# The sums of four adaLN vectors on GpSimd in 512-column pieces, instead of VectorE in 1024-column pieces

## The chip, the cores and the metric

The kernel runs on one core of a Trainium2 chip. The metric is the device time of one execution in microseconds (us). Engines are named as in the profile: PE is TensorE, DVE is VectorE, ACT is ScalarE, POOL is GpSimd, and SP is the engine whose queue issues most DMAs.

## What is computed

One decoder layer for 256 tokens of 2048 channels, all in float32. Six adaLN vectors are one product of a conditioning vector with a 2048 x 12288 matrix; they shift, scale and gate the two sub-layers.

```python
mod = c_act @ w_mod[l].astype(f32) + b_mod[l].astype(f32)
shift1, scale1, gate1, shift2, scale2, gate2 = [t[:, None, :] for t in jnp.split(mod, 6, axis=-1)]
u = _rms(h, norm1_w[l]) * (1.0 + scale1) + shift1
proj = u @ w_in[l].astype(f32)
...
merged = (jax.nn.sigmoid(gate_a) * (o_a @ p_a[l].astype(f32))
          + jax.nn.sigmoid(gate_b) * (o_b @ p_b[l].astype(f32)))
h = h + gate1 * (merged @ w_out[l].astype(f32))
u = _rms(h, norm2_w[l]) * (1.0 + scale2) + shift2
ff = jax.nn.silu(u @ w_gate[l].astype(f32)) * (u @ w_up[l].astype(f32))
h = h + gate2 * (ff @ w_down[l].astype(f32))
```

`o_a` is the output of a stick-breaking attention, `o_b` that of a gated DeltaNet (a chunked recurrence with a triangular solve).

## The kernel before

All large products stream their weights. `run_jobs` goes through 648 steps of one block each: 256 rows by 512 columns of a weight matrix, 512 KB, in a tile `raw` (four buffers) that SP's queue loads. ACT rounds a block to float32r (`wh`), DVE takes the rest (`wl`, one subtraction of two SBUF tiles), and PE adds three products for each pair of parts into `acc`. ACT and DVE prepare a block three steps ahead (`SA`); the load of the block four further on is written behind `wl`, since it takes that block's buffer. A job has the activations as the stationary side (12 products of 512 columns in a step) or, with `chan`, the weights (24 products of 256 columns).

Between the products run smaller chains. The first third of the program is the gated DeltaNet (`gdn_chain`, `conv_chain`), whose many small steps on DVE, ACT and PE hang on one another, with four POOL steps for each group of heads for inverse roots (`rr`, `sso`); then comes the attention (`sb_chain`), then the output products, then the FFN.

Shift1 and scale1 are summed at the start and don't change here. The other four vectors are background tasks: shift2 (index 3), scale2 (4), gate1 (2), gate2 (5). `run_jobs` counts ticks, two in a step, and calls `pump_bg` for one background step every `bg_every` ticks, in the first call only from tick `bg_from`. In `mod_steps` a background step loads the next piece of `w_mod` (128 rows by 1024 columns, tile `wm`, 512 KB, two buffers) on SP's queue and adds the piece at hand, times its value of silu(c), to the accumulator `macc` on DVE (L120, in the helper `stt`; the first piece L194). One vector takes 32 pieces; four vectors 128. Then PE sums over partitions: `mod_cols` by transposes and sums on ACT, `mod_bcast` by two products with ones after a split on ACT and DVE.

The order in which each engine's queue holds its instructions is set ahead of the run by a scheduler that follows the program's order and its own forecast of when an instruction can start; on the chip each queue is strictly in that order.

Of the kernel before, what the change touches and what calls it, by code (L numbers as in the profile page):

```python
# [16 lines left out]
P = 128  # L17
# [9 lines left out]
RAWS = 4  # L27
MW = 1024
GROUPS = (0, 2, 1, 3)
# [4 lines left out]
NZ = 3  # L34
BGF = 200
BGE = 3
H2 = 5
# [56 lines left out]
def body(tc, cst, x, c, w_mod, b_mod, norm1_w, w_in, q_norm_w, k_norm_w, conv_w, a_log, dt_bias,  # L94
# [32 lines left out]

    # constants
    cs0 = cp.tile([P, 2 * P], F32, name="cs0")
# [40 lines left out]

    # adaLN vectors
    def mod_steps(i, acc, pool, width, bufs, row, cc=cc):
        v0 = i * D
        if row:
            nc.gpsimd.memset(acc, 0.0)
            nc.sync.dma_start(out=acc[0:1], in_=b_mod[v0:v0 + D].rearrange("(o d) -> o d", o=1))
        parts = [(k, j) for k in range(KT) for j in range(0, D, width)]
        tiles = {}

        def load(n):  # L180
            k, j = parts[n]
            t = pool.tile([P, width], F32, tag="mraw", name=f"wm{i}_{n}", bufs=bufs)
            nc.sync.dma_start(out=t, in_=w_mod[k * P:(k + 1) * P, v0 + j:v0 + j + width])
            tiles[n] = t

        load(0)
        for n, (k, j) in enumerate(parts):
            if n + 1 < len(parts):
                load(n + 1)
            t = tiles.pop(n)  # L190
            if k or row:
                stt(acc[:, j:j + width], t, cc[:, k:k + 1], acc[:, j:j + width], ALU.mult, ALU.add)
            else:
                nc.vector.tensor_scalar(out=acc[:, j:j + width], in0=t, scalar1=cc[:, 0:1], scalar2=None, op0=ALU.mult)  # L194
            yield

    def mod_cols(acc, o, bias):
        for j in range(4):
            b = bank("pb_mod")
            for i in range(4):  # L200
                tr(b[:, i * P:(i + 1) * P], acc[:, (4 * j + i) * P:(4 * j + i + 1) * P])
            for i in range(4):
                k = 4 * j + i
                # in place: only the sum is used
                act(b[:, i * P:(i + 1) * P], b[:, i * P:(i + 1) * P], AF.Copy, accum_out=o[:, k:k + 1])
            yield
        tt(o, o, bias, ALU.add)
        yield

    def mod_bcast(acc, o, pool):  # L210
        for j in range(4):
            sl = slice(j * 512, (j + 1) * 512)
            hi = pool.tile([P, 512], F32R, tag="c2", name="bch", bufs=4)
            lo = pool.tile([P, 512], F32R, tag="c2", name="bcl", bufs=4)
            nc.scalar.copy(out=hi, in_=acc[:, sl])
            tt(lo, acc[:, sl], f32(hi), ALU.subtract)
            yield
            b = bank("pb_bc")
            mm(b, onesr, hi, True, False)
            mm(b, onesr, lo, False, True)  # L220
            nc.scalar.copy(out=o[:, sl], in_=b)
            yield

    # chains of small steps that run between the products of the streams
    chains = deque()
# [39 lines left out]

    # streamed products: float32 operands as exact sums of two float32r parts
    def run_jobs(jobs, bg_every=0, outer=(), bg_from=0):
# [30 lines left out]
        for n, (j, q) in enumerate(steps):  # L298
# [14 lines left out]
            def beat(t):  # L313
                # between the products of half a k-step
                if own:
                    if t == SPA and n + SA < ns:
                        split_hi(n + SA)
                    if t == SPB and n + SA < ns:
                        split_lo(n + SA)
                    pump_conv()  # L320
                    pump(j.pump)
# [36 lines left out]

# [1 line left out]
    acc01 = big.tile([P, 2, D], F32, tag="s16", name="acc01")  # L360
# [8 lines left out]
    def load_smod(n):  # L369
        # shift1 and scale1  # L370
        for i in [i for i in loads if i not in smod][:max(0, n - len([i for i in smod if smod[i] is not None]))]:
            pi, g = i
            k0, kn = pieces[pi]
            c0, cn = k0 * P, kn * P
            kg = 4 // kn
            t = tps.tile([P, 2, kg, cn], F32, tag="smod", name="smod", bufs=SMB)
            src = w_mod[g * kg * P:(g + 1) * kg * P, 0:2 * D].rearrange("(k p) (v n) -> p v k n", p=P, v=2)
            if kg == 1:
                nc.gpsimd.dma_start(out=t[:, :, 0], in_=src[:, :, 0, c0:c0 + cn])
            else:  # L380
                for v in range(2):
                    nc.gpsimd.dma_start(out=t[:, v], in_=src[:, v, :, c0:c0 + cn])
            smod[i] = t
# [78 lines left out]

    # the modulated input, 512 channels at a time as the columns of w_mod come in
    def u_piece(pi):
# [26 lines left out]

# [1 line left out]
    def gdn_scalars():  # L493
# [60 lines left out]

    # steps of the tensor engine for one group of four heads by slot; the digit: chunk of 128 rows
    def gdn_slots():
# [27 lines left out]
    def gdn_chain(g, tl):  # L584
# [7 lines left out]
        U = sysv(wB[:, 0])  # L592
        # two systems side by side: their even blocks on 64 partitions each
        Tm = sysv(wB[:, 1, 0:512])
# [18 lines left out]
        hold = {}  # L613
        # blocks of 16 on the diagonal: their places in turn, then system, on partitions; columns and rows free
        Lt, Tt = wA[:, 0, 0:512], wA[:, 0, 512:1024]
# [16 lines left out]
        def gather():  # L632
            # of each 32 the two blocks' columns over one another
            for q in range(4):
                e = slice(32 * q, 32 * q + 32)
                j = 32 * q
                nc.scalar.copy(out=Lc[e], in_=L[e, :, j:j + BW])
                nc.vector.copy_predicated(out=Lc[e], mask=mk["par"][e, 1:2].bitcast(mybir.dt.uint32).unsqueeze(2).to_broadcast([32, 8, BW]),
                                          data=L[e, :, j + BW:j + 2 * BW])
# [6 lines left out]
        def stages(j0, j1):  # L646
            # in place: row j of the inverse is done, its part in the rows below
            for j in range(j0, j1):
                n = BW - 1 - j
                t = tmp[:, 0:2 * n * j].rearrange("p (c h r) -> p c h r", h=2, r=n)  # L650
                tt(t, Tb[:, j, :, j + 1:].unsqueeze(1).to_broadcast([P, j, 2, n]),
                   Tb[:, 0:j, :, j].unsqueeze(3).to_broadcast([P, j, 2, n]), ALU.mult)
                d = Tb[:, 0:j, :, j + 1:]
                tt(d, d, t, ALU.add)
# [12 lines left out]
        def take_even(c):  # L667
            # the even blocks' columns of L
            s = LEVELS[level[c]]
# [3 lines left out]
        def turn(c, part):  # L673
            # the even blocks of T, their rows in order without the odd ones
            s = LEVELS[level[c]]
# [10 lines left out]
        def step(op, c):  # L686
# [53 lines left out]
            if op == "KK":  # L740
# [4 lines left out]
                def lower():  # L745
                    # L holds minus the strict part (its upper part is not used)
                    for h, s in enumerate(sys):
                        stt(L[:, s], ph(b, h), nbrk2[:, s:s + 1], Dm[:, s], ALU.mult, ALU.mult)
# [45 lines left out]
            if op == "Y":  # L794
                # the last level: two blocks of 64
                b = bank("pb_X")
# [121 lines left out]

    # the first halves of the second group's sums wait in SBUF for the rest of the input
    part = []  # L920
# [45 lines left out]

# [1 line left out]
    oa = {}  # L968
# [121 lines left out]

    # adaLN vectors of the second half
    def mod_col_task(i, slot):
        acc = tph["tp"].tile([P, D], F32, tag="macc", name="macc", bufs=1)
        yield from mod_steps(i, acc, tph["tp"], MW, 2, False)
        yield from mod_cols(acc, mcols[:, slot], {3: bsh2, 4: bsc2}[i])

# [3 lines left out]

# [1 line left out]
    def z_done(n):  # L1102
# [109 lines left out]

# [1 line left out]
    def gate_task(i, key, cc):  # L1214
        acc = tq.tile([P, D], F32, tag="macc2", name="macc2", bufs=1)
        yield from mod_steps(i, acc, tq, 1024, 2, True, cc)
        st[key] = tq.tile([P, D], F32, tag="gbc", name=key, bufs=1)
        yield from mod_bcast(acc, st[key], tq)

# [21 lines left out]

# [1 line left out]
    def ffn_begin():  # L1243
# [15 lines left out]
        norm_apply(hn, mcols[:, 2], b2, st["u2h"], st["u2l"])  # L1259
        # silu(c) again, in the place of b2: gate2's sums come after the norm  # L1260
        cc2 = cp.tile([P, KT], F32, tag="gate", name="cc2", bufs=1)
# [86 lines left out]

    run_jobs(jobs, bg_every=6)
    drain()  # L1350
# [24 lines left out]
```

## Time and profile before

| what | value |
|---|---|
| time, median of 3 runs | 2090.61 us (2089.65, 2090.61, 2098.76) |
| span of the profiled execution | 2093.9 us, from its first to its last instruction |
| profiled execution's own time | not listed apart from its span |
| PE busy | 2003.8 us (96%) |
| DVE busy | 1351.5 us (65%) |
| ACT busy | 1033.3 us (49%) |
| POOL busy | 115.5 us (6%) |
| HBM read | 445.70 MB, 214 GB/s over the span |

A matmul's end is modelled in the profile, so PE counts as busy almost always; whether it runs at its pace is read from how many products fall in a stretch. The chain that ended last lies for 78% on PE and for 9% on DMA.

### The profile page before, as it was taken

How to read it: one execution, taken by the hardware profiler on the slowest of the kernel's cores; microseconds unless marked ns; L12 is line 12 of the kernel's file. 1: busy time of each engine (PE TensorE's matmuls, PEld its weight loads, DVE VectorE, ACT ScalarE, POOL GpSimd, SP SyncE). 2: the span in 40 equal slices, each digit the busy share in tenths (PEclk: the TensorE clock that was granted, in tenths of full speed). 3: DMA queues.
4: the chain of work that ended last, by engine and by line, in shares of the span. 5: the costliest groups of instructions: out<-in, count | busy, mean ns of one | idle time of the engine just before them, and what ended most of it. 6: DMA issues, size and time to landing. Idle time of an engine off the chain costs nothing.

```text
span 2093.9 us, 31884 instructions
## 1 busy us (share of the span) xinstructions
PE 2003.8 (96%) x12505; PEld 1795.5 (86%) x12505; DVE 1351.5 (65%) x1758; ACT 1033.3 (49%) x1678; POOL 115.5 (6%) x139
## 2 busy tenths in 40 slices
PE   1999999999999999999999999999999999999998
PEld 1899999987888788877888888898999889999987
DVE  4987989987558876667654555677545454445454
ACT  3346676675666567433454444533444333444432
POOL 4411011110000000000000000000000000000000
PEclk9899999999999999999999999999999999999999
DMA  8995664664658875888766665688666556666664
GB/s 308 386 333 183 188 200 123 192 206 148 188 164 264 294 225 153 261 290 289 224 190 192 189 218 192 194 296 280 209 183 181 188 194 187 186 183 181 185 211 138
DMA packets 208561, 449.90 MB, mean 215 GB/s; under 512 B 16101, under 2 KB 16536, under 8 KB 207896
## 3 DMA queue, kind: packets, MB, share of 16 engines
q1 hardware_dynamic: 198906, 413.25, 63.3%
q0 software_dynamic: 9504, 34.61, 4.4%
q8 instruction: 98, 1.61, 0.3%
q14 instruction: 53, 0.43, 0.1%
HBM read 445.70 MB, written 2.10 MB: 214 GB/s over the span
## 4 chain that ended last, share of the span: by engine, by line
PE 78%; DMA 9%; DVE 6%; issue 3%; ACT 3%; SPq 0%; POOL 0%; DVEq 0%; ACTq 0%
PE acc L114 71%; DMA wm<-in_w_mod 7%; DVE wl L117 2%; DMA crow<-in_conv_w 1%; DVE macc L120 1%; ACT wh L282 1%; DMA smod<-in_w_mod 1%; PE pb_mod L114 1%; PE pb_Q L114 1%; PE pb_u L136 1%; DMA raw<-in_w_in 0%; PE pb_X L114 0%; PE pb_z L114 0%; PE pb_oa L114 0%; DVE gw L117 0%
## 5 line engine op out<-in xcount | busy, mean ns | idle before, releaser
L117 DVE TENSOR_TENSOR wl<-raw,wh 128x1024 fp32r<-128x1024 f32 x648 | 789.6, 1223 | 516.5 <-ACT wh L282 514.6
L282 ACT CAST wh<-raw 128x1024 fp32r<-128x1024 f32 x648 | 679.6, 1050 | 834.0 <-PE acc L114 670.1
L114 PE MATMUL acc<-u2h,wl 128*128 128x256 f32 x1408 | 399.3, 284 | 4.9 <-DVE wl L117 4.9
L114 PE MATMUL acc<-u2h,wh 128*128 128x256 f32 x1408 | 398.5, 283 | 0.0
L114 PE MATMUL acc<-u2l,wh 128*128 128x256 f32 x1408 | 398.4, 283 | 0.0
L114 PE MATMUL acc<-wh,uh 128*128 128x512 f32 x768 | 307.1, 400 | 0.0
L114 PE MATMUL acc<-wl,uh 128*128 128x512 f32 x768 | 301.2, 392 | 2.0 <-DVE wl L117 2.0
L114 PE MATMUL acc<-wh,ul 128*128 128x512 f32 x768 | 300.2, 391 | 0.0
L114 PEld LDWEIGHTS acc<-u2h,wl 128*128 128x128 f32 x1408 | 270.2, 192 | 6.2 <-DVE wl L117 6.1
L114 PEld LDWEIGHTS acc<-u2h,wh 128*128 128x128 f32 x1408 | 270.3, 192 | 0.0
L114 PEld LDWEIGHTS acc<-u2l,wh 128*128 128x128 f32 x1408 | 270.3, 192 | 0.0
L114 PE MATMUL acc<-uh,wh 128*128 128x256 f32 x768 | 220.9, 290 | 1.6 <-ACT part L927 1.3
L114 PE MATMUL acc<-uh,wl 128*128 128x256 f32 x768 | 219.4, 287 | 0.0
L114 PE MATMUL acc<-ul,wh 128*128 128x256 f32 x768 | 219.0, 286 | 0.0
L114 PE MATMUL acc<-wh,ff 128*128 128x512 f32 x704 | 217.1, 389 | 0.0
L114 PEld LDWEIGHTS acc<-wl,uh 128*128 128x128 f32 x768 | 144.4, 188 | 34.5 <-DVE wl L117 4.1
L114 PEld LDWEIGHTS acc<-wh,ul 128*128 128x128 f32 x768 | 144.8, 189 | 27.2
L114 PEld LDWEIGHTS acc<-wh,uh 128*128 128x128 f32 x768 | 144.9, 189 | 26.8
L120 DVE SCALAR_TENSOR_TENSOR macc<-wm,cols,macc 128x1024 f32<-128x1024 f32 x92 | 117.8, 1283 | 65.7 <-DMA wm<-in_w_mod 65.2
L114 PEld LDWEIGHTS acc<-wh,ff 128*128 128x128 f32 x704 | 132.1, 188 | 27.3
L114 PEld LDWEIGHTS acc<-uh,wh 128*128 128x128 f32 x768 | 148.7, 195 | 2.8 <-ACT part L927 1.5
L114 PEld LDWEIGHTS acc<-ul,wh 128*128 128x128 f32 x768 | 149.3, 194 | 0.5
(289 smaller groups left out, 2493.1 us busy)
## 6 DMA issues: line engine op xcount, KB each, us to landing
raw<-in_w_in SPq DMA_DIRECT2D x286, 512.0 KB, 4.5
wm<-in_w_mod SPq DMA_DIRECT2D x128, 512.0 KB, 5.3
raw<-in_w_gate SPq DMA_DIRECT2D x88, 512.0 KB, 3.9
raw<-in_w_up SPq DMA_DIRECT2D x88, 512.0 KB, 3.7
raw<-in_w_down SPq DMA_DIRECT2D x88, 512.0 KB, 3.9
smod<-in_w_mod POOLq DMA_DIRECT2D x64, 512.0 KB, 11.2
raw<-in_p_a SPq DMA_DIRECT2D x32, 512.0 KB, 5.6
raw<-in_p_b SPq DMA_DIRECT2D x32, 512.0 KB, 4.0
```

Source lines behind the costliest of these rows:

```text
L114: nc.tensor.matmul(o, lhsT=lhsT, rhs=rhs, start=start, stop=stop, skip_group_check=True)
L117: nc.vector.tensor_tensor(out=o, in0=a, in1=b, op=op)
L120: nc.vector.scalar_tensor_tensor(out=o, in0=a, scalar=s, in1=b, op0=op0, op1=op1, **kw)
L136: nc.tensor.transpose(o, i, ident)
L282: nc.scalar.copy(out=wh, in_=raws[n])
```

## The change

`mod_steps` is replaced by `mod_parts`. A vector is summed 512 columns at a time: for each quarter of the columns all 16 row blocks, so that one vector takes 64 pieces of 256 KB, and four vectors 256. The accumulator is 128x512 with two buffers. A piece is multiplied by its value of silu(c) in place and then added, both on POOL (`tensor_scalar`, `tensor_tensor`). Loads run four pieces ahead (`MRA`) with six buffers (`MRB`). The sum over partitions of a quarter (`use`) follows its 16 pieces. The first call of `run_jobs` now pumps every two ticks from tick 80 (was three, from 200), the second every three (was six). The products, their splits and the loads of `raw` are as before; comments went too.

```diff
-MW = 1024
-BGF = 200
-BGE = 3
+BGF = 80
+BGE = 2
+BGD = 3
+MRA = 4
+MRB = 6
...
-    def mod_steps(i, acc, pool, width, bufs, row, cc=cc):
+    def mod_parts(i, pool, row, cc, use):
         v0 = i * D
-        if row:
-            nc.gpsimd.memset(acc, 0.0)
-            nc.sync.dma_start(out=acc[0:1], in_=b_mod[v0:v0 + D].rearrange("(o d) -> o d", o=1))
-        parts = [(k, j) for k in range(KT) for j in range(0, D, width)]
+        parts = [(q, k) for q in range(4) for k in range(KT)]
         tiles = {}
 
         def load(n):
-            k, j = parts[n]
-            t = pool.tile([P, width], F32, tag="mraw", name=f"wm{i}_{n}", bufs=bufs)
-            nc.sync.dma_start(out=t, in_=w_mod[k * P:(k + 1) * P, v0 + j:v0 + j + width])
+            q, k = parts[n]
+            t = pool.tile([P, 512], F32, tag="mraw", name=f"wm{i}", bufs=MRB)
+            nc.sync.dma_start(out=t, in_=w_mod[k * P:(k + 1) * P, v0 + q * 512:v0 + (q + 1) * 512])
             tiles[n] = t
 
-        load(0)
-        for n, (k, j) in enumerate(parts):
-            if n + 1 < len(parts):
-                load(n + 1)
+        for n in range(MRA):
+            load(n)
+        for n, (q, k) in enumerate(parts):
+            if n + MRA < len(parts):
+                load(n + MRA)
+            if k == 0:
+                acc = pool.tile([P, 512], F32, tag="macc", name="macc", bufs=2)
+                if row:
+                    nc.gpsimd.memset(acc, 0.0)
+                    nc.sync.dma_start(out=acc[0:1], in_=b_mod[v0 + q * 512:v0 + (q + 1) * 512].rearrange("(o d) -> o d", o=1))
             t = tiles.pop(n)
-            if k or row:
-                stt(acc[:, j:j + width], t, cc[:, k:k + 1], acc[:, j:j + width], ALU.mult, ALU.add)
-            else:
-                nc.vector.tensor_scalar(out=acc[:, j:j + width], in0=t, scalar1=cc[:, 0:1], scalar2=None, op0=ALU.mult)
+            first = k == 0 and not row
+            nc.gpsimd.tensor_scalar(out=acc if first else t, in0=t, scalar1=cc[:, k:k + 1], scalar2=0.0,
+                                    op0=ALU.mult, op1=ALU.add)
+            if not first:
+                nc.gpsimd.tensor_tensor(out=acc, in0=acc, in1=t, op=ALU.add)
             yield
...
-    run_jobs(jobs, bg_every=6)
+    run_jobs(jobs, bg_every=BGD)
```

The new order of the queues shows at three places. The first is SP's queue at the start of the DeltaNet, behind the load of the constants `cs`: `raw` is a streamed block, `wm` a piece of `w_mod`. Before:

```order
L183 DMA wm_0_5081<-in_w_mod 128x1024
L277 DMA raw<-in_w_in 128x2x512
L183 DMA wm_1_5083<-in_w_mod 128x1024
L277 DMA raw<-in_w_in 128x2x512
L183 DMA wm_2_5154<-in_w_mod 128x1024
L277 DMA raw<-in_w_in 128x2x512 x2
L183 DMA wm_3_5204<-in_w_mod 128x1024
L277 DMA raw<-in_w_in 128x2x512
L183 DMA wm_4_5262<-in_w_mod 128x1024
L277 DMA raw<-in_w_in 128x2x512 x16
```

A part of the same stretch of SP's queue in the changed kernel:

```order
L289 DMA raw<-in_w_in 128x2x512 x2
L182 DMA wm_2650<-in_w_mod 128x512
L182 DMA wm_2690<-in_w_mod 128x512
L182 DMA wm_2736<-in_w_mod 128x512
L182 DMA wm_2785<-in_w_mod 128x512
L182 DMA wm_2823<-in_w_mod 128x512
L182 DMA wm_2898<-in_w_mod 128x512
L182 DMA wm_2932<-in_w_mod 128x512
L182 DMA wm_2966<-in_w_mod 128x512
L289 DMA raw<-in_w_in 128x2x512
```

Eight loads of pieces now stand between two loads of blocks. From the first piece on, 13 block loads have 37 piece loads among them, where before 13 block loads had 5.

The second place is POOL's queue a little further on, with `rr` the inverse roots of the DeltaNet. In the changed kernel:

```order
L197 TENSOR_SCALAR wm_2898<-wm_2898,cols 128x512
L200 TENSOR_TENSOR macc<-macc,wm_2823 128x512
L197 TENSOR_SCALAR wm_2932<-wm_2932,cols 128x512
L200 TENSOR_TENSOR macc<-macc,wm_2898 128x512
L197 TENSOR_SCALAR wm_2966<-wm_2966,cols 128x512
L171 TENSOR_TENSOR rr<-rr,half 128x4
L200 TENSOR_TENSOR macc<-macc,wm_2932 128x512
L200 TENSOR_TENSOR macc<-macc,wm_2966 128x512
L197 TENSOR_SCALAR wm_3000<-wm_3000,cols 128x512
L171 TENSOR_TENSOR rr<-rr,half 128x4
```

Before, POOL's queue held no `wm` at all. The third place is SP's queue in the first product after the attention (`p_a`), while gate1 is summed. Before:

```order
L277 DMA raw<-in_p_a 128x2x512
L183 DMA wm_17_10102<-in_w_mod 128x1024
L277 DMA raw<-in_p_a 128x2x512 x2
L183 DMA wm_18_10159<-in_w_mod 128x1024
L277 DMA raw<-in_p_a 128x2x512
L183 DMA wm_19_10220<-in_w_mod 128x1024
```

The same product in the changed kernel:

```order
L289 DMA raw<-in_p_a 128x2x512
L182 DMA wm_10769<-in_w_mod 128x512
L182 DMA wm_10801<-in_w_mod 128x512
L289 DMA raw<-in_p_a 128x2x512
L182 DMA wm_10835<-in_w_mod 128x512
L289 DMA raw<-in_p_a 128x2x512
L182 DMA wm_10863<-in_w_mod 128x512
L182 DMA wm_10897<-in_w_mod 128x512
L289 DMA raw<-in_p_a 128x2x512
```

Two pieces, then one, now stand between blocks: 54 piece loads among 42 block loads in this product and the stretch ahead of it. For gate2, at the start of the FFN, it is 58 among 38.

## Rows read from the trace of the kernel before

**Rows 1.** The page's span, and its first part: busy us, share, instructions.

```profile
span 2093.9 us, 31884 instructions
PE 2003.8 (96%) x12505; PEld 1795.5 (86%) x12505; DVE 1351.5 (65%) x1758; ACT 1033.3 (49%) x1678; POOL 115.5 (6%) x139
```

**Rows 2.** Windows, all engines: start:end, length, then as the first line says.

```profile
core 0: us, PE busy (x) PEld busy (x) DVE busy (x) ACT busy (x) POOL busy (x), PEclk, DMA share, GB/s
165.00:515.00 350.00, 334.00 (x2677) 313.95 (x2676) 308.39 (x675) 235.35 (x574) 36.33 (x37) 0.99 0.60 181
```

**Rows 3.** Windows, PE's products into `acc` alone: busy us and their number.

```profile
640.00:755.00 115.00, 101.03 (x414) 0.99 0.87 291
755.00:860.00 105.00, 97.41 (x408) 1.00 0.63 178
860.00:1000.00 140.00, 133.14 (x569) 1.00 0.88 292
1100.00:1150.00 50.00, 50.00 (x222) 1.00 0.65 196
1340.00:1465.00 125.00, 120.10 (x989) 1.00 0.87 291
1500.00:1550.00 50.00, 50.00 (x419) 1.00 0.63 186
```

**Rows 4.** Windows, DVE's instructions on `macc` alone: busy us and their number.

```profile
165.00:515.00 350.00, 39.82 (x32) 0.99 0.60 181
640.00:755.00 115.00, 39.11 (x31) 0.99 0.87 291
860.00:1000.00 140.00, 39.83 (x31) 1.00 0.88 292
1340.00:1465.00 125.00, 41.68 (x34) 1.00 0.87 291
```

**Rows 5.** Waits, whole span (us in total, times, longest); then 165 to 515 us.

```profile
DVE macc L120 <- DMA wm<-in_w_mod: 96.3, 70, 3.7
...
  DMA wm<-in_w_mod: 10.7, 7
```

**Rows 6.** Groups of instructions on POOL: busy us, mean ns | idle before.

```profile
L619 POOL MEMSET gw<- 128x1024 f32 x4 | 3.8, 951 | 134.9 <-PE pb_u L114 59.1 <-ACT wh L282 50.0 <-PE pb_mod L114 25.4
L623 POOL MEMSET gw<- 128x512 f32 x4 | 2.1, 526 | 0.0
L1250 POOL COPY b<-mcols 128x16 f32<-128x16 f32 x1 | 0.7, 650 | 31.6 <-DVE mcols L117 31.6
```

**Rows 7.** Timeline, three stretches: start, duration, instruction [idle before].

```profile
199.72 1.23 DVE L117 TENSOR_TENSOR wl<-raw,wh 128x1024 fp32r<-128x1024 f32 x1
199.90 1.94 POOL L169 TENSOR_TENSOR rr<-rr,half 128x4 f32<-128x4 f32 x1 [36.84 <-DVE rr L713]
...
1337.58 1.22 DVE L117 TENSOR_TENSOR wl<-raw,wh 128x1024 fp32r<-128x1024 f32 x1
1337.73 1.72 POOL L1262 COPY cc<-cols 128x16 f32<-128x16 f32 x1 [11.19 <-DVE uf L1278]
...
292.05 0.48 DVE L120 SCALAR_TENSOR_TENSOR gv<-acc,cw,gv 128x254 f32<-128x254 f32 x1
292.22 1.01 POOL L169 TENSOR_TENSOR rr<-rr,half 128x4 f32<-128x4 f32 x1 [0.35 <-DVE rr L713]
```

**Rows 8.** Groups on DVE by shape, 165 to 515 us.

```profile
L117 DVE TENSOR_TENSOR wl<-raw,wh 128x1024 fp32r<-128x1024 f32 x85 | 103.8, 1221 | 5.6 <-ACT wh L282 4.3 <-ACT gw L780 0.7
L683 DVE STREAM_TRANSPOSE gw<-gw 32x64 f32<-32x64 f32 x96 | 22.5, 235 | 2.6 <-ACT gw L123 1.3
L117 DVE TENSOR_TENSOR Gh<-cs,gth 128x512 fp32r<-128x512 f32 x8 | 5.5, 686 | 0.0
```

**Rows 9.** Timeline of SP's queue, start of the DeltaNet.

```profile
182.78 0.46 SPq L183 DMA_DIRECT2D wm<-in_w_mod  x1
188.22 47.71 SPq L277 DMA_DIRECT2D raw<-in_w_in  x16
```

More of the change, by code (lines that the diff above doesn't have):

```diff
@@ L195, in mod_steps, with mod_cols, use @@
             yield
-    def mod_cols(acc, o, bias):
-        for j in range(4):
+            if k == KT - 1:
+                yield from use(q, acc)
+    def mod_cols(i, o, bias, pool, cc):
+        def use(q, acc):
             b = bank("pb_mod")
[L200 to L205, printed above, removed]
+            for n in range(4):
+                tr(b[:, n * P:(n + 1) * P], acc[:, n * P:(n + 1) * P])
+            for n in range(4):
+                k = 4 * q + n
+                act(b[:, n * P:(n + 1) * P], b[:, n * P:(n + 1) * P], AF.Copy, accum_out=o[:, k:k + 1])
@@ L206, in mod_cols, with mod_bcast, use @@
             yield
+        yield from mod_parts(i, pool, False, cc, use)
         tt(o, o, bias, ALU.add)
         yield
-    def mod_bcast(acc, o, pool):
-        for j in range(4):
-            sl = slice(j * 512, (j + 1) * 512)
+    def mod_bcast(i, o, pool, cc):
+        def use(q, acc):
+            sl = slice(q * 512, (q + 1) * 512)
             hi = pool.tile([P, 512], F32R, tag="c2", name="bch", bufs=4)
             lo = pool.tile([P, 512], F32R, tag="c2", name="bcl", bufs=4)
-            nc.scalar.copy(out=hi, in_=acc[:, sl])
-            tt(lo, acc[:, sl], f32(hi), ALU.subtract)
+            nc.scalar.copy(out=hi, in_=acc)
+            tt(lo, acc, f32(hi), ALU.subtract)
@@ L222, in mod_bcast @@
             yield
+        yield from mod_parts(i, pool, True, cc, use)
     chains = deque()
@@ L1092, in mod_col_task @@
     def mod_col_task(i, slot):
-        acc = tph["tp"].tile([P, D], F32, tag="macc", name="macc", bufs=1)
-        yield from mod_steps(i, acc, tph["tp"], MW, 2, False)
-        yield from mod_cols(acc, mcols[:, slot], {3: bsh2, 4: bsc2}[i])
+        yield from mod_cols(i, mcols[:, slot], {3: bsh2, 4: bsc2}[i], tph["tp"], cc)
     background.append(mod_col_task(3, 3))
@@ L1214, in gate_task @@
     def gate_task(i, key, cc):
-        acc = tq.tile([P, D], F32, tag="macc2", name="macc2", bufs=1)
-        yield from mod_steps(i, acc, tq, 1024, 2, True, cc)
         st[key] = tq.tile([P, D], F32, tag="gbc", name=key, bufs=1)
-        yield from mod_bcast(acc, st[key], tq)
+        yield from mod_bcast(i, st[key], tq, cc)
     background.append(gate_task(2, "g1", cc))
```

## The prediction

> **What bounds the kernel now.** I read the page's busy times first [rows 1]: PE is busy for 2003.8 of 2093.9 us, so little is to be had unless PE runs below its pace while it counts as busy. For that I counted its products by stretch [rows 3]. Undisturbed, 222 products of 512 columns take 50 us (0.2252 us each, 2.70 us for a step of 12), and 419 of 256 columns take 50 us (0.1193 us each, 2.86 us for a step of 24). Then I looked at where DVE adds pieces of w_mod [rows 4]: four stretches hold nearly all of them, and in them DVE waits 96.3 us in total for pieces that have not landed [rows 5], with `wl` queued behind. There the products come too slowly. At 860 to 1000 us (gate1), 569 products should take 128.1 us and take 140: 11.9 us lost. At 1340 to 1465 us (gate2), 989 should take 118.0 and take 125: 7.0 lost. At 640 to 755 us (attention, scale2), 414 at the pace of the stretch behind it (105 us for 408) should take 106.5 and take 115: 8.5 lost. The DeltaNet, 165 to 515 us, is different [rows 2]: DVE is busy for 308 of 350 us and PE for 334, so PE could give back 16 us at most, and DVE's work is what stands closest in its way.
>
> **What the change removes.** In the DeltaNet 39.8 us of DVE's time on pieces [rows 4] and 10.7 us of waits for them [rows 5], 50.5 us together. In the three later stretches the losses above, 27.4 us, in so far as nothing takes their place. The bytes are the same, and the transposes and products that sum over partitions are the same in number; the smaller splits (8 of 128x512) stay on ACT and DVE.
>
> **What it adds: the price of a piece on POOL.** No row shows a `tensor_scalar` or an add of 512 columns on POOL. From below, a MEMSET of this shape takes 0.526 us, and 512 columns more cost 0.425 us [rows 6], so the two instructions take 1.05 us at least. From above, a COPY of only 16 columns takes 0.650 us where it meets nothing [rows 6]; with 496 columns more at 0.83 ns it would be 1.06 us, and with a second input of 512 columns 1.49 us: 2.55 us for a piece. I take 1.7 us, just under the middle, as POOL's rows of wide shapes lie nearer the lower end. The GPSIMD Engine Reference of the Trainium skill (Performance versus the Vector engine) gives 4497 ns for an add of 2048 columns, by which one of 512 would be an estimated 1.12 us and the sum below some 2147 us; no run here shows it.
>
> **What it collides with.** POOL's small steps show who blocks whom. An inverse root of 128x4 takes 1.01 us alone [rows 7]. The one at 199.90 us started 0.18 us into a `wl` and took 1.94 us: it ended 0.89 us after `wl` did. The COPY of 16 columns at 1337.73 us, again inside a `wl`, took 1.72 us instead of 0.65. The root at 292.22 us, inside an instruction of DVE that reads `acc` in PSUM, was not held. So a POOL instruction that reads SBUF waits until DVE's instruction with two SBUF inputs is done. I assume the reverse too: while POOL reads, such an instruction of DVE waits. The rows cannot show that, as POOL now reads only 4 to 16 columns. The Trainium skill says the same (SBUF — State Buffer, Who interferes with whom): the pair is an exclusive lock and "the other fully blocks"; the trace agrees for POOL's half, by the 0.9 us above. The sum by this rule is the sum below; without it, it is the first rival.
>
> Every `wl` has two SBUF inputs, one of 1.22 us in each step, and so do many DeltaNet steps (`Gh`); the transposes and those that read PSUM are free of it [rows 8].
>
> **The sum, stretch by stretch.** *DeltaNet.* Where before 32 pieces were added [rows 4] (34 loaded), the new order of SP's queue has 102 loaded. They hold the port for 102 x 1.7 = 173 us. About half of DVE's time there is in instructions with two SBUF inputs (`wl` alone 104 of 350 us [rows 8], all some 175), so I let half of POOL's time block DVE: 87 us, against 50.5 removed, 36 us more. Some of it falls into DVE's 42 idle us [rows 2], so I count two thirds: +24 us. Bounds: a gain of 16 (PE's idle time), or 102 x 2.55 / 2 - 50.5 = +80. Within this lies a stall at its start: 13 block loads there have 37 piece loads among them, and the 37th needs 31 pieces finished (six buffers). At 1.7 us that is 53 us; 13 blocks went out in about 39 us before, at the pace of the 16 in 47.7 us [rows 9].
>
> *Attention.* All of scale2's loads now stand ahead of it: -8.5 us.
>
> *Gate1.* SP's queue has 54 pieces among 42 blocks. A piece load waits for POOL to free a buffer and holds the block loads behind it, so POOL's pace becomes PE's. A step needs the port for 1.22 + 54/42 x 1.7 = 3.41 us, over the step's 2.70: 0.71 x 42 = 30 us, less the three steps (8 us) that are split ahead, is 22. Against the 11.9 lost before: +10 us. Bounds: with 1.05 us a piece the port fits (2.57), -12; with 2.55 it takes 4.50, +56.
>
> *Gate2.* 58 pieces among 38 blocks: 1.22 + 58/38 x 1.7 = 3.81 us in a step of 2.86: 36 us, less 9 split ahead, is 27, against 7.0: +20 us. Bounds: -7 and +70.
>
> Sum: 24 - 8.5 + 10 + 20 = +45.5 us. The profile's span is 3.3 us over the median of the three runs, which is the spread between runs, so I add the change to the median: 2090.6 + 45.5 = **2136 us**. All lower bounds together give 2090.6 - 43.5 = 2047, all upper ones 2288.
>
> **The rivals.** *First, faster: POOL does not hold DVE back.* If POOL's reads do not block DVE, or a piece costs POOL near 1.05 us, the losses go (27.4 us) and the DeltaNet gives back up to 16: 2047 to 2080 us, with 2056 for most of it. For it speaks that only POOL's waiting stands in the rows, and that DVE has much idle time in gate1 and gate2. Against it, 199.90 us shows one resource that two engines take in turn. It decides from about 1.1 us a piece, where the port fits in gate1's step.
>
> *Second, no change.* DVE's waits go and the port's come, about equal, as with 1.4 us a piece: 2080 to 2101 us.
>
> *Third, much slower: POOL's backlog.* At 2.55 us a piece POOL is late everywhere. Block loads wait behind piece loads, and the roots `rr`, on which the DeltaNet hangs, stand behind pieces in POOL's queue. 2190 to 2288 us.
>
> **The numbers.** The forecast, DVE and POOL in each other's way at 1.5 to 2.1 us a piece, gets 0.58, with 2101 to 2190 us of its own; the first rival 0.25, the second 0.11, the third 0.06. The range of 2050 to 2190 us leaves out the third rival, the fastest fifth of the first and a tenth of the forecast, under 0.2. A measurement of this kernel tells a change of 0.5% (10.5 us) from none: faster 0.25, same 0.13 (the second rival and the forecast's low end), slower 0.62.
>
> **What would show it.** Right: `wl` still near 1.22 us alone, but with stretches of 0.4 to 1 us added to it or idle ahead of it wherever POOL works; POOL's two instructions for a piece taking together clearly more than they do in a stretch where DVE reads PSUM; products in gate1 and gate2 below 222 and 419 in 50 us while pieces are added; SP waiting for POOL ahead of piece loads; the DeltaNet's end later than 515 us. Wrong: `wl` unchanged and unhindered beside POOL's adds; gate1 and gate2 at full pace; the DeltaNet ending by 515 us. The step most likely to fail is the one that rests on no row: that DVE waits for POOL, and how long.

## The result and the profile after

The changed kernel takes 2241.43 us (median of 4 runs, 2241.06 to 2243.27) against 2093.88 us for the kernel before on the same chip: ratio 1.0711, 95% interval [1.0689, 1.0733]. It is slower by 148 us (149 by the ratio), above the range.

The page of the changed kernel: span, busy times, chain, groups (busy us, mean ns of one).

```profile
span 2239.3 us, 32484 instructions
PE 2036.3 (91%) x12505; PEld 1822.3 (81%) x12505; DVE 1309.9 (58%) x1630; ACT 1034.9 (46%) x1678; POOL 751.6 (34%) x649
...
PE 54%; POOL 16%; issue 2%; DMA 1%; DVE 1%; ACT 1%; SPq 0%; DVEq 0%; ACTq 0%; POOLq 0%
...
L119 DVE TENSOR_TENSOR wl<-raw,wh 128x1024 fp32r<-128x1024 f32 x648 | 848.0, 1313 | 645.4 <-ACT wh L294 637.6
...
L200 POOL TENSOR_TENSOR macc<-macc,wm 128x512 f32<-128x512 f32 x248 | 384.2, 1549 | 17.7 <-DMA macc<-in_b_mod 0.7
```

POOL, with 0% of the chain before, holds 16% of it. The same instructions by tile (minimum/median/maximum ns):

```profile
L200 POOL TENSOR_TENSOR macc<-macc,wm x248: 1252/1292/2363, 176.2 to 1627.4; 128x512 f32<-128x512 f32 x124
L197 POOL TENSOR_SCALAR wm<-wm,cols x184: 682/695/2747, 175.5 to 1210.5; 128x512 f32<-128x512 f32 x184
```

A piece that meets nothing takes 0.69 + 1.29 = 1.98 us. The mean is 1.55 for the add and 1.02 (`cols`) to 1.10 (`cc`) for the product, so 2.57 us, just over the prediction's upper bound of 2.55. Windows: all engines from 165 to 515 us (as in [rows 2]), then PE's products into `acc` alone in two other stretches (as in [rows 3]), and POOL's instructions on pieces alone in these two.

```profile
165.00:515.00 350.00, 282.21 (x2284) 271.71 (x2283) 260.05 (x516) 187.04 (x471) 203.97 (x186) 0.90 0.52 163
```

```profile
956.00:1112.00 156.00, 139.27 (x578) 0.96 0.73 243
1460.00:1622.00 162.00, 129.38 (x1006) 0.88 0.68 225
```

```profile
956.00:1112.00 156.00, 131.58 (x99) 0.96 0.73 243
1460.00:1622.00 162.00, 155.22 (x119) 0.88 0.68 225
```

In the first of these windows, of the DeltaNet, 2284 products run where 2677 ran before [rows 2]. Less work falls into it, so DVE's 260 us against 308 don't tell how long its instructions take. The same work in both kernels is steps 32 to 160 of the table below. There, all engines before, DVE's instructions on `macc` before, all engines after:

```profile
167.26:653.29 486.03, 470.03 (x3315) 427.51 (x3314) 389.09 (x785) 325.30 (x784) 46.67 (x47) 0.99 0.60 181
167.26:653.29 486.03, 45.10 (x37) 0.99 0.60 181
168.37:756.12 587.75, 493.75 (x3315) 445.07 (x3314) 414.23 (x747) 328.50 (x799) 340.12 (x295) 0.91 0.56 173
```

Without its pieces DVE is busy for 389.1 - 45.1 = 344.0 us there before and for 414.2 in the change: the same instructions take 70.2 us more. Its idle time grows too, from 96.9 to 173.5 us. At gate1 578 products at the pace of 0.2252 us should take 130.2 us and take 156; at gate2 1006 at 0.1193 should take 120.0 and take 162. POOL works on pieces for 132 of the 156 us and for 155 of the 162. SP's queue at the start of the DeltaNet (timeline; as in [rows 9]):

```profile
182.14 14.07 SPq L182 DMA_DIRECT2D wm<-in_w_mod  x7
196.32 0.89 SPq L289 DMA_DIRECT2D raw<-in_w_in  x2
197.93 15.55 SPq L182 DMA_DIRECT2D wm<-in_w_mod  x8
213.57 0.39 SPq L289 DMA_DIRECT2D raw<-in_w_in  x1
215.16 2.34 SPq L182 DMA_DIRECT2D wm<-in_w_mod  x2
217.61 0.38 SPq L289 DMA_DIRECT2D raw<-in_w_in  x1
219.74 13.39 SPq L182 DMA_DIRECT2D wm<-in_w_mod  x6
233.24 0.38 SPq L289 DMA_DIRECT2D raw<-in_w_in  x1
```

Between 182 and 233 us five block loads go out; before, 16 went out in 47.7 us [rows 9]. The waits of the whole span (total us, times, longest), SP's queue first, then the engines:

```profile
SPq L182 <- POOL macc L200: 369.1, 212, 5.3
```

```profile
ACT wh L294 <- DMA raw<-in_w_in: 125.0, 55, 9.1
...
ACT bch L225 <- POOL macc L200: 72.4, 5, 20.2
DVE bcl L119 <- ACT bch L225: 67.9, 5, 18.8
...
DVE sso L122 <- POOL sso L171: 39.4, 4, 16.8
DVE co L119 <- POOL rr L171: 31.1, 4, 13.6
```

A late POOL reaches the products by three ways: SP's queue (a piece load that waits for a buffer stands ahead of block loads, so `wh` waits for `raw`), the roots `rr` and `sso` behind pieces in POOL's queue, and the splits `bch`, `bcl` of a finished vector, which stand in ACT's and DVE's queues ahead of the next `wh` and `wl`. The port shows too, in this timeline of the FFN:

```profile
1497.56 2.71 POOL L197 TENSOR_SCALAR wm<-wm,cc 128x512 f32<-128x512 f32 x1
...
1499.84 1.50 DVE L119 TENSOR_TENSOR wl<-raw,wh 128x1024 fp32r<-128x1024 f32 x1
...
1500.36 2.14 POOL L200 TENSOR_TENSOR macc<-macc,wm 128x512 f32<-128x512 f32 x1
...
1502.47 0.69 POOL L197 TENSOR_SCALAR wm<-wm,cc 128x512 f32<-128x512 f32 x1
...
1502.73 1.51 DVE L119 TENSOR_TENSOR wl<-raw,wh 128x1024 fp32r<-128x1024 f32 x1 [1.39 <-ACT wh L294]
```

Here `wl` takes 1.5 us, not 1.22, and the add 2.14, not 1.29. Over the span `wl` takes 848.0 us, against 648 x 1.223 = 792.5 at its pace alone (the mean of the kernel before). All of DVE's work without pieces grows from 1351.5 - 161.7 = 1189.8 us to 1309.9 (its groups on pieces took 117.8, 40.9 and 3.0 before).

The stages, each from the start of the `wl` of one step to that of another in the traces' timelines (us), for before, after and the runs below that tell them apart. Steps 32 to 160 are the DeltaNet and the head of the attention, 224 to 272 hold most of gate1's pieces, 392 to 432 those of gate2.

| kernel | 32-160 | 160-224 | 224-272 | 272-392 | 392-432 | 432-640 |
|---|---|---|---|---|---|---|
| before | 486.0 | 205.7 | 145.4 | 344.8 | 122.0 | 588.2 |
| after | 587.7 | 199.9 | 155.9 | 348.5 | 161.4 | 583.4 |
| paced | 539.2 | 201.3 | 131.7 | 349.0 | 115.7 | 594.2 |
| gpin | 588.3 | 199.9 | 131.9 | 348.6 | 115.6 | 594.5 |
| writesp | 509.7 | 199.6 | 130.6 | 348.3 | 115.7 | 588.0 |
| hold5 | 534.3 | 199.6 | 139.8 | 352.8 | 115.7 | 588.0 |
| rootsp | 523.3 | 199.6 | 131.9 | 347.4 | 115.6 | 594.2 |
| poolq | 602.0 | 199.7 | 161.5 | 351.1 | 175.1 | 588.0 |
| dve512 | 483.8 | 199.6 | 130.5 | 347.6 | 115.4 | 588.0 |
| writes | 499.9 | 199.9 | 130.6 | 348.0 | 115.6 | 588.0 |
| write1 | 485.3 | 199.6 | 130.6 | 347.4 | 115.6 | 588.0 |

After less before: +101.7, -5.8, +10.5, +3.7, +39.4, -4.8.

### The profile page after: what moved, and what is told of

It reads as the page before. It is cut to its first block, busy times and chain, and to the rows that moved or that the text cites. A ratio compares the mean times of both kernels' runs of the same rounds, so it can differ in the third digit from the quotient of the medians.

```text
span 2239.3 us, 32484 instructions
## 1 busy us (share of the span) xinstructions
PE 2036.3 (91%) x12505; PEld 1822.3 (81%) x12505; DVE 1309.9 (58%) x1630; ACT 1034.9 (46%) x1678; POOL 751.6 (34%) x649
## 4 chain that ended last, share of the span: by engine, by line
PE 54%; POOL 16%; issue 2%; DMA 1%; DVE 1%; ACT 1%; SPq 0%; DVEq 0%; ACTq 0%; POOLq 0%
PE acc L116 52%; POOL macc L200 10%; POOL wm L197 6%; DVE wl L119 1%; ACT wh L294 0%; DMA raw<-in_w_in 0%; PE pb_z L116 0%; PE pb_oa L116 0%; PE pb_af L116 0%; DMA raw<-in_w_up 0%; PE pb_sq L138 0%; PE pb_tr L138 0%; DMA wm<-in_w_mod 0%; DMA macc<-in_b_mod 0%; DMA raw<-in_p_a 0%
## 5 line engine op out<-in xcount | busy, mean ns | idle before, releaser
L119 DVE TENSOR_TENSOR wl<-raw,wh 128x1024 fp32r<-128x1024 f32 x648 | 848.0, 1313 | 645.4 <-ACT wh L294 637.6
L200 POOL TENSOR_TENSOR macc<-macc,wm 128x512 f32<-128x512 f32 x248 | 384.2, 1549 | 17.7 <-DMA macc<-in_b_mod 0.7
L116 PE MATMUL acc<-uh,wh 128*128 128x256 f32 x768 | 225.7, 297 | 1.3 <-ACT part L939 1.0
L197 POOL TENSOR_SCALAR wm<-wm,cols 128x512 f32<-128x512 f32 x184 | 187.4, 1023 | 85.9 <-DMA wm<-in_w_mod 85.9
L116 PEld LDWEIGHTS acc<-uh,wl 128*128 128x128 f32 x768 | 152.2, 199 | 7.6 <-DVE wl L119 7.2
```

The lines of the kernel that those rows point to most:

```text
L116: nc.tensor.matmul(o, lhsT=lhsT, rhs=rhs, start=start, stop=stop, skip_group_check=True)
L119: nc.vector.tensor_tensor(out=o, in0=a, in1=b, op=op)
L197: nc.gpsimd.tensor_scalar(out=acc if first else t, in0=t, scalar1=cc[:, k:k + 1], scalar2=0.0, op0=ALU.mult, op1=ALU.add)
L200: nc.gpsimd.tensor_tensor(out=acc, in0=acc, in1=t, op=ALU.add)
```

## The experiments

The first theory (queue, later backlog): the scheduler placed the loads and what depends on POOL too early for POOL's real pace, and what stands behind it waits. Its rival (port): POOL's reads and DVE's instructions with two SBUF inputs shut each other out, in any order. Ratios are to the kernel before on the same chip.

**The order of SP's queue alone (paced).** Loads of pieces, biases and blocks in the order in which the program writes them.

```diff
-nc.sync.dma_start(out=t, in_=w_mod[...])
+tc.keep_in_program_order(nc.sync.dma_start(out=t, in_=w_mod[...]))
...
-queue.dma_start(out=r, in_=j.w[...])
+tc.keep_in_program_order(queue.dma_start(out=r, in_=j.w[...]))
```

> The changed kernel with SP's queue pinned to the program's order: about one piece load for each block load in the DeltaNet and 0.67 later, where the changed kernel has up to eight in a row. POOL's work and its reads are the same. Queue theory (block loads and roots wait behind pieces that run at POOL's pace, 2.6 us each): most of the 147 us goes, 2095 to 2140 us, and SP waits for POOL ahead of piece loads for under 100 us instead of 385. Port theory (POOL's reads hold up DVE's two-input instructions, whatever the order): the same 256 pieces cost the same, 2200 us or more.

2135.56 us, ratio 1.0199 [1.0178, 1.0221]. Some 107 us of the loss are gone with the same reads on POOL, and SP's waits for POOL's buffers fall from some 390 us to 22. Both gates are now ahead of the kernel before; what is left lies in steps 32 to 160 (+53.2). There the port stays busy, as these groups of its page show (`wl` 1313 ns and the add 1549 in the change), and its window of steps 32 to 160:

```profile
L119 DVE TENSOR_TENSOR wl<-raw,wh 128x1024 fp32r<-128x1024 f32 x648 | 871.3, 1347 | 599.0 <-ACT wh L294 596.1
...
L200 POOL TENSOR_TENSOR macc<-macc,wm 128x512 f32<-128x512 f32 x248 | 404.5, 1631 | 19.2
```

```profile
169.29:708.50 539.21, 486.85 (x3315) 439.24 (x3315) 428.03 (x747) 328.07 (x800) 324.32 (x262) 0.96 0.59 181
```

DVE is busy for 428.0 us there, 84.0 more than before without pieces and 13.8 more than in the change. So the 48.5 us by which the change is slower than paced in these steps are not longer instructions of DVE; they go with the order of the loads.

**The reads away (writesp).** The ordered queue, each piece four fills of 512 columns on POOL.

```diff
-            nc.gpsimd.tensor_scalar(out=acc if first else t, in0=t, ...)
-            if not first:
-                nc.gpsimd.tensor_tensor(out=acc, in0=acc, in1=t, op=ALU.add)
+            nc.gpsimd.memset(t, 0.0)
+            for _ in range(3):
+                nc.gpsimd.memset(acc, 0.0)
```

> As paced, with the same order of SP's queue, but each piece's multiply and add on POOL are four MEMSETs of 512 columns (about 1.9 us, which write and do not read SBUF), so the four vectors are not summed. Port theory: DVE's subtraction returns to 1.223 us on average and the time falls well below paced, by 50 us or more. Queue theory: within 15 us of paced, since pace and order are nearly the same.

2096.49 us, ratio 1.0018 [1.0008, 1.0027]: 39 us below paced, between the two expectations. Its `wl` is back at its pace:

```profile
L119 DVE TENSOR_TENSOR wl<-raw,wh 128x1024 fp32r<-128x1024 f32 x648 | 791.4, 1223 | 673.0 <-ACT wh L293 672.0
```

POOL's writes don't hold `wl`; its reads do. But the writes hold other instructions of DVE. A single wait of PE for `gt`, of 16.3 us, is in this run and not in paced. It comes from `gs<-gs`, a small step of DVE with one SBUF input, which stands ahead of `gt` in DVE's queue:

```profile
177.72 22.03 POOL L199 MEMSET macc<- 128x512 f32 x47
...
182.22 17.56 DVE L516 TENSOR_SCALAR gs<-gs 128x32 f32<-128x32 f32 x1
```

It took 0.17 us in the kernel before; here it ends 0.03 us after the last of 47 fills that ran without a break. So fills are no neutral stand-in, and without this wait the reads would cost up to 16 us more than the 39.

**DVE in the ordered queue (dve512p).** As paced, each piece one fused product and add on DVE (`stt`).

> As paced, with the same order of SP's queue, but each piece is multiplied and added in one instruction on DVE. Four pieces ahead, 512 columns, no POOL. Both theories: the waits for w_mod (96 us of DVE in the kernel before) nearly vanish; DVE works 256 x 0.69 = 177 us on pieces instead of 167. Estimate 2065 to 2095 us, at or below the kernel before. If it is above 2110, the structure (512 columns, quarters, earlier start) costs by itself.

2099.91 us, ratio 1.0039 [1.0027, 1.0052], some 5 us above what was expected. DVE waits 158.2 us (91 times) for pieces that have not landed: in the program's order the loads come late for a fast summing engine.

**The roots (roots, rootsp, and the control broots).** The inverse roots as reciprocals on DVE, in the changed kernel, in paced and in the kernel before.

```diff
-        nc.gpsimd.tensor_tensor(out=o, in0=i, in1=half[:, 0:o.shape[-1]], op=ALU.pow)
+        nc.vector.reciprocal(out=o, in_=i)
```

> The changed kernel with the inverse roots replaced by reciprocals on DVE (other values, same shapes), so that they don't stand behind pieces in POOL's queue; SP's order is as in the changed kernel to within two loads. Queue theory: DVE's 70 us of waits for POOL in the DeltaNet go, and 40 to 70 us of the time with them, 2170 to 2200 us; what stays is block loads behind piece loads. Port theory: at most 20 us less, 2220 to 2241 us.

> The change with the ordered queue, and the inverse square roots taken from GpSimd as reciprocals on DVE (other values). It tells whether the 39 us that the ordered queue leaves are DVE and GpSimd lengthening each other or roots that wait behind pieces. The port theory: what is left lies in the reads, so no better than the ordered queue with the roots on GpSimd, 2130 to 2145 us. The backlog theory: the roots' waits of about 18 us end, 2105 to 2125 us.

> The kernel before with its inverse square roots taken from GpSimd as reciprocals on DVE (other values): the control for the two runs that did so. If those won 34 and 20 us because the roots stood behind pieces on GpSimd, nothing of it is to be had here, where GpSimd has no pieces: 2085 to 2095 us. If the root on GpSimd is dear by itself: 2060 to 2075 us.

roots: 2207.27 us, 1.0550 [1.0531, 1.0569], 34 us below the change, between the two expectations. rootsp: 2115.5 us, 1.0109 [1.0089, 1.0129], 19 us below paced by the ratios. broots: 2085.55 us, 0.9957 [0.9936, 0.9978], 9 us gained where POOL has no pieces. So roots behind pieces cost about 25 us in the change (34 - 9) and 10 in the ordered queue (19 - 9). They seem to have no part in the 39 us between paced and writesp: the waits for `rr` and `sso` are as long in both (18.1 us in paced, 8.1 and 10.0; 19.6 in writesp, 11.0 and 8.6).

**The gate stage alone in order (gpin).** DeltaNet's order unchanged; `keep_in_program_order` for the loads of the second `run_jobs`.

> The change with its own order of loads through DeltaNet, bit for bit, and the ordered queue in the gate stage alone. GpSimd reads as much as in the change. The backlog theory: the gate stage (steps 224 to 432) goes from 665.8 us to the 596.4 us of the ordered kernel and DeltaNet keeps its loss (587.7 us from step 32 to 160), so 2241 less 69: 2172 us (2160 to 2185). The port theory: the gate pieces' reads cost what they cost in any order, 2225 us or more.

2183.09 us, 1.0426 [1.0405, 1.0447]. Steps 32 to 160 keep their 588.3 us, the gates fall to the ordered kernel's 131.9 and 115.6. This window of gate2's stretch shows POOL at work and PE at its pace (834 products in 100 us, as 419 in 50 [rows 3]):

```profile
1460.00:1560.00 100.00, 100.00 (x834) 99.92 (x833) 59.97 (x46) 41.74 (x46) 62.27 (x46) 1.00 0.72 233
```

So the loss of these steps goes with the order. Gate2's stage in this run has 56 instructions of POOL on pieces where the change has 119 in its window:

```profile
1437.20:1552.80 115.60, 78.97 (x56) 1.00 0.73 239
```

That the reads cost nothing holds for this density, not for the change's. There some 59 pieces would keep POOL busy for 117 us at 1.98 us each, hardly more than PE's 115.6; at the port they became 155. Order and port both have a hand in it. Behind step 432, where the ordered queue puts gate2's last pieces, 594.5 us stand against 588.2 before: some 6 us.

**Gates alone on POOL, or on DVE (gpool, gdve).** The kernel before with gate1 and gate2 by `mod_parts` and the ordered queue in that stage; shift2 and scale2 stay on DVE in 1024 columns.

```diff
-        yield from mod_steps(i, acc, tq, 1024, 2, True, cc)
-        yield from mod_bcast(acc, st[key], tq)
+        yield from mod_bcast(i, st[key], tq, cc)
...
-    run_jobs(jobs, bg_every=6)
+    run_jobs(jobs, bg_every=BGD, pin=True)
```

> The kernel before, with shift2 and scale2 left on DVE inside DeltaNet as they were, and only the two gate vectors on GpSimd (512 columns, four ahead) with SyncE's loads of pieces and blocks in program order. The queue theory: the loss of the change lies in DeltaNet, and the gate stage (weight-load steps 224 to 432) took 612.2 us before and 596.4 us with the ordered queue, so some 16 us below the kernel before: about 2077 us (2070 to 2085). The port theory: GpSimd's reads lengthen DVE's weight work here as they do in DeltaNet, by 128 of the 248 pieces of the ordered kernel's 39 us or more, so 2095 to 2115 us.

> As the run beside it, but the gate pieces are summed by DVE (512 columns, four ahead). Tells whether a gain of the gate stage comes from GpSimd's hands or from the loads that run four ahead. If from the loads: the ordered kernel with the pieces on DVE took 602.2 us from step 224 to 432 against 612.2 before, so about 2082 us (2075 to 2090). If from GpSimd's hands alone: 2090 to 2095 us, no change.

gpool: 2083.74 us, 0.9967 [0.9954, 0.9979]. gdve: 2087.6 us, 0.9979 [0.9969, 0.9989]. Half the change, in order, is a small gain, some 7 us with POOL adding and 4 with DVE. So more than half of it seems to come from the loads four ahead, whoever adds; the two intervals overlap.

**The scheduler's order with DVE adding (dve512).** The changed kernel's loads, tiles and pumps; `stt` on DVE.

```diff
-            nc.gpsimd.tensor_scalar(out=acc if first else t, in0=t, ...)
-            if not first:
-                nc.gpsimd.tensor_tensor(out=acc, in0=acc, in1=t, op=ALU.add)
+            if first:
+                nc.vector.tensor_scalar(out=acc, in0=t, scalar1=cc[:, k:k + 1], scalar2=None, op0=ALU.mult)
+            else:
+                stt(acc, t, cc[:, k:k + 1], acc, ALU.mult, ALU.add)
```

> The change with its loads, tiles and order, but the pieces are summed by DVE in one fused operation each. Loads in SyncE's queue stand as far ahead as the scheduler puts them. The queue theory as GpSimd's backlog: without a late GpSimd the queue's order alone costs little, 2095 to 2120 us. If the order of the loads alone costs what the change lost, whoever sums: 2180 us or more. The port theory: GpSimd reads nothing of the pieces, 2100 us.

2071.81 us, 0.9902 [0.9889, 0.9916]: the best kernel of the study, and better than either theory gave. Its groups on DVE:

```profile
L119 DVE TENSOR_TENSOR wl<-raw,wh 128x1024 fp32r<-128x1024 f32 x648 | 790.9, 1222 | 520.3 <-ACT wh L294 518.5
...
L122 DVE SCALAR_TENSOR_TENSOR macc<-wm,cols,macc 128x512 f32<-128x512 f32 x184 | 137.4, 747 | 28.5 <-DMA wm<-in_w_mod 24.1
```

A piece takes 0.75 us on DVE against 2.57 on POOL, and the waits for pieces fall to 38.2 us (96.3 before, [rows 5]). In the gate stage its order of loads is nearly the change's (153 piece loads ahead of block 240, 200 ahead of 392 and 256 ahead of 432 in both), and gate2 takes 115.4 us instead of 161.4. So that order is no fault in itself: it gains where the adding engine keeps up. In the DeltaNet the scheduler orders the two kernels differently (13 piece loads ahead of block 50, against 38), so there the pair is less clean.

**Piece loads on POOL's own queue (poolq).**

```diff
-            nc.sync.dma_start(out=t, in_=w_mod[...])
+            nc.gpsimd.dma_start(out=t, in_=w_mod[...])
```

> The change as it is, but its piece loads are issued on GpSimd's queue and no longer on SyncE's, so a block load can't stand behind a piece load; GpSimd still reads as much, and pays some 0.74 us more for each of the 252 loads that it issues. The queue theory: most of the 106 us that the ordered queue gave back comes back here too, less what the issues cost where GpSimd is late: 2140 to 2190 us. The port theory, in which GpSimd's own reads hold the weight work: no better than the change, 2225 us or more.

2281.02 us, 1.0907 [1.0892, 1.0921]: a miss for the queue theory as it stood. POOL pays 0.58 us for each of 256 issues and is later still, and the products find it by another way. ACT's timeline at gate2:

```profile
1588.82 1.05 ACT L294 CAST wh<-raw 128x1024 fp32r<-128x1024 f32 x1 [1.83 <-PE acc L116]
1616.84 0.62 ACT L225 CAST bch<-macc 128x512 fp32r<-128x512 f32 x1 [26.97 <-POOL macc L200]
1617.37 2.94 ACT L294 CAST wh<-raw 128x1024 fp32r<-128x1024 f32 x3
```

ACT's queue stands for 27 us at a split whose vector isn't summed, with three `wh` behind it. So the theory is one of backlog, not of SP's queue alone.

**Lateness without reads (writes, write1, hold5).** The change's kernel with the scheduler's order. writes has writesp's edit, write1 one fill a piece, hold5 five fills of the piece's own buffer:

```diff
+            for _ in range(5):
+                nc.gpsimd.memset(t, 0.0)
+            if first:
+                nc.gpsimd.memset(acc, 0.0)
```

> The change with its loads in the order that the scheduler chooses, but each piece on GpSimd is four fills of 512 columns (2.1 us) that read nothing, so the four vectors aren't summed. The backlog theory: GpSimd is late by the time of its pieces whatever they read, and what waits behind it stands still: 2150 to 2210 us. The port theory: with no reads by GpSimd beside DVE nothing is lost, 2070 to 2100 us. If the order of the loads alone costs: as the run beside it, which has the same order.

> As the run beside it, with one fill (0.53 us) a piece in place of four, and nearly the same order of loads (128 of the piece loads stand ahead of block load 88 in SyncE's queue in both); the vectors aren't summed. The backlog theory: GpSimd keeps up, so 2055 to 2090 us. The port theory: the same as the run beside it, 2060 to 2100 us for both. If the order of the loads alone costs, whoever keeps up: both over 2130 us.

> The change with the scheduler's own order of loads, but each piece on GpSimd is five fills of the piece's own buffer (2.64 us, against a mean of 2.57 us for the change's piece), which hold that buffer as long as the change's two operations do and read nothing; the vectors aren't summed. The fills of the run writes could be moved ahead of their loads, so its GpSimd wasn't late where the change's is; these can't. The backlog theory: GpSimd as late as in the change costs without any read, above all from step 32 to 160, which took 587.7 us against 486.0 before: 530 us or more there, 2120 to 2200 us in all. The port theory: without reads 485 to 510 us there, 2065 to 2100 us in all.

writes: 2097.28 us, 1.0010 [0.9989, 1.0032], a miss for the backlog theory; write1: 2070.27 us, 0.9895 [0.9876, 0.9913]. In writes (2084.07 to 2101.43 us) the fills of `acc` hang on no load, and its trace shows them far ahead of their pieces (11 before the first piece, later over 200 between two), so POOL was less late than meant. In hold5 they can't run ahead: 2133.1 us (2115.9 to 2134.75), 1.0171 [1.0129, 1.0213], with 534.3 us from step 32 to 160, inside what the backlog theory expected. Its waits of SP's queue and its `wl`:

```profile
SPq L182 <- POOL wm L198: 351.2, 222, 6.2
```

```profile
L119 DVE TENSOR_TENSOR wl<-raw,wh 128x1024 fp32r<-128x1024 f32 x648 | 792.0, 1224 | 720.3 <-ACT wh L294 715.8
```

`wl` is untouched and 48.3 us are lost in steps 32 to 160 all the same. But that isn't lateness alone, for the fills hold DVE as in writesp:

```profile
180.81 20.60 POOL L198 MEMSET wm<- 128x512 f32 x44
...
181.72 19.74 DVE L517 TENSOR_SCALAR gs<-gs 128x32 f32<-128x32 f32 x1
```

The step `rr<-rr` ahead of the roots takes up to 4.36 us there instead of 0.17, and DVE is busy for 386.1 us, 42.1 more than before without pieces. How much of the 48.3 is lateness stays open.

The clean case is gate1's stage. In it hold5 and writes have nearly the same order (195 and 198 piece loads ahead of block 272), `wl` is at its pace in both, and only hold5's POOL is late. First `wl` alone in hold5 and in writes, then hold5's waits in its window:

```profile
901.00:1041.00 140.00, 59.04 (x49) 1.00 0.88 291
868.00:998.00 130.00, 58.34 (x48) 1.00 0.94 325
```

```profile
SPq L182 <- POOL wm L198: 84.5, 57, 2.9
```

```profile
ACT wh L294 <- DMA raw<-in_p_a: 43.6, 22, 3.3
```

The stage takes 139.8 us in hold5 and 130.6 in writes: 9.2 us by lateness alone.

## Why the prediction was wrong

The direction was right, the size a third of what came. What happened is the third rival, with 0.06 the least likely of all.

- **The price of a piece.** I took 1.7 us, "just under the middle, as POOL's rows of wide shapes lie nearer the lower end". Those rows are fills, which read nothing; a piece reads three times. Measured: 1.98 us alone, 2.57 us with its waits. The figure of the GPSIMD Engine Reference of the Trainium skill (Performance versus the Vector engine), an estimated 1.12 us for the add, is below the 1.25 us of the fastest one here. The sum of 2147 us that goes with it comes out only with 0.65 us for the product, which the prediction doesn't name. The sum asks for the time at the port, so 1.98 belongs in it. That makes it +87 instead of +45.5 us, 2177 us, still inside the range: the price alone isn't what failed.
- **DeltaNet, +24 us: the step that failed.** Measured is +101.7 us from step 32 to 160, beyond even the bound of +80. I let POOL's pieces block DVE for 87 us, set 50.5 us of removed work against that, counted two thirds of the rest, and took the stall at the start as lying "within this", at no price.
  - The block came about as large as I took it: DVE's instructions take 70.2 us more in the change and 84.0 in paced.
  - The credit did not come, as far as runs with orders of their own can show it. In write1 DVE adds no piece, POOL spends a fill of 0.53 us on each, and the stage takes 485.3 us against 486.0 before; in dve512 DVE adds every piece, and it takes 483.8. DVE's pieces were not what held the stage up, so taking them away gave next to nothing. Two thirds of 87 without the credit are 58, near the 53.2 that paced loses with its loads in order.
  - The stall was not within this: the scheduler's order costs the other 48.5 us (the change less paced). The first burst alone (steps 32 to 48) takes 89.0 us against 57.8, +31, and 63.6 in paced, and it comes again with later bursts of loads and with roots. I had the order's rows, 37 piece loads among 13 block loads and the roots behind pieces, and priced them at nothing beside the port. Since each run has an order of its own, this is no exact split. That lateness costs without any read is shown only in gate1's stage (9.2 us, hold5); how much of the 48.5 is lateness by itself and how much pieces crowded at the port stays open.
- **Attention, -8.5 us.** -5.8 from step 160 to 224. Right.
- **Gate1, +10 us.** +10.5, right in size by luck: with 1.98 us a piece my sum would have given +25. Gpin, with another order and a third of the pieces in this stage, ends 13.5 us ahead of the kernel before in it.
- **Gate2, +20 us.** +39.4. With 1.98 us a piece the sum gives +36.5, so the term was mis-sized by its price. I had let POOL and DVE take turns at the port, and the stages fit that: 48 `wl` of 1.22 us and 49 pieces of 1.98 one after another would take 156 us at gate1, 40 and 59 would take 166 at gate2; the stages take 155.9 and 161.4. With gpin's 16 and 28 pieces the turns would take 91 and 104 us, less than PE needs, and nothing is lost. This fit is a sum, no experiment.
- **The rivals.** The first (POOL doesn't hold DVE) is refuted in its condition: `wl` and the adds do lengthen each other. The Trainium skill's rule that I drew on (SBUF — State Buffer, Who interferes with whom) is borne out in both halves. But the rule says who waits, not what that costs: where the pieces were spread and PE was the bound (gpin's gates) it cost nothing, in the DeltaNet 30 us (paced less writesp), or 46 if the wait that writesp's fills cause is set aside.

Of the 148 us, about 107 go with the order in which the loads stand relative to a late POOL (paced). The 42 that stay with the loads in order go, but for 4, with POOL's reads (writesp). Roots behind pieces are about 25 of the whole, 10 of them among those 42. What also stays open is how much of the DeltaNet's loss is PE's clock: its mean there is 0.90 of 2.4 GHz, where it was 0.99 [rows 2], so PE, with its stalls, spent part of the stretch at 1.2 GHz; no run separates the slower clock from the stalls.

## What to carry to other kernels

Work moved to an idle engine is free only if that engine keeps its date: list everything that waits for it in any in-order queue (loads of its buffers, its own small steps on a critical chain, the use of its result in other engines' queues) and hold its real price against the forecast by which the order was made. Price an engine's operation by a row that reads as it reads; a fill is no stand-in for an add, and as a control it holds the neighbour in its own way. Credit work taken from an engine only if the stage would have ended sooner without it. Change the look-ahead and the engine apart: here smaller pieces, begun earlier and loaded further ahead, were worth 1% (dve512), and the move to POOL cost 8% on top.

## What the runs showed of the hardware

- POOL's reads and DVE's subtraction of two SBUF tiles lengthen each other: `wl` 1.22 us alone and 1.35 on average in paced, the add 1.29 alone and up to 2.36, the product 0.69 alone and up to 2.75.
- POOL's fills leave that subtraction alone: with up to 602 us of them in the span (hold5), `wl` stays at 1.224 us. But DVE's small `tensor_scalar` with one SBUF input waits for a break between them: `gs<-gs` of 128x32, 0.17 us before, took 17.56 us beside 47 fills in a row (writesp) and 19.74 us beside 44 (hold5).
- Both engines lose by the reads: POOL's pieces took 650 us in the change against 248 x 1.292 + 256 x 0.695 = 498 at their medians, 152 lost; DVE's work without pieces grew by 120 us, of which `wl` has 55.5.
- A DMA issued by POOL costs it 0.58 us (poolq), an issue on SP's queue 0.33.
